# Layer 1 of a two-layer decoder: the low activations beside the high ones, one 512-column product with the high weights

## The chip, the core and the metric

The kernel runs on one core of a Trainium2 chip. TensorE (PE in the profile; its weight loads are PEld) multiplies, VectorE (DVE), ScalarE (ACT) and GpSimd (POOL) do the elementwise work, SyncE (SP) issues most DMAs. The metric is the device time in microseconds (us). Before the change it is 2330.26 us, the median of three runs (2329.82 to 2330.46).

## The reference

One sequence of 256 tokens, 16 meta tokens put in front (272 rows in all), width 2048, two layers, float32. Layer 0 works on all 272 rows. In layer 1 the shared K and V are made from all 272 rows, while queries, attention output and MLP are wanted for the 256 real tokens alone, since the output drops the meta rows.

```python
for layer in range(DEPTH):
    a = rms_norm(h, norm_attn[layer])
    if layer < N_A_LAYERS:
        ...
        o = forgetting_attention(split_heads(q), split_heads(k), split_heads(v), cum_logf)
        h = h + o.reshape(b, length, D_MODEL) @ fox_w_o[i]
    else:
        ...
        q = split_heads(a @ sb_w_q[i])
        o = stick_breaking_attention(q, shared_k, shared_v)
        h = h + o.reshape(b, length, D_MODEL) @ sb_w_o[i]
    h = h + squared_relu_mlp(rms_norm(h, norm_mlp[layer]), w_up[layer], w_down[layer])
return rms_norm(h, final_norm)[:, N_META:]
```

## The kernel before

Activations lie feature-major: 16 chunks of 128 features, each chunk 272 tokens wide (layer 1: 256). A float32 product is made of three products in the rounded type fp32r: an operand is split into a high part (ScalarE copies it into fp32r) and a low part (VectorE subtracts the high part from the original), and the kernel sums high weights x high activations, high weights x low activations, and low weights x high activations. The split of activations lives in a `Split` object: one SBUF tile with a row of 640 columns for each chunk, `hi` and `lo` views in it. `ROWS` says where in the row they start: for layer 1 (`t0 = M = 16`) hi at column 0 and lo at column 320.

Every weight matrix is worked off by `gemm_group` in column blocks of 512: four PSUM tiles `acc_<group>_<m>`, one whole bank each (512 float32 columns), for m = 0..3 of 128 output features. A group runs over four blocks kb of 512 input features. For each kb it loads two halves of raw weights (`raw`, on SP's queue), ScalarE makes `whi` (L222) and VectorE `wlo` (L223), each half 128 x 1024; `whi` and `wlo` have four buffers each, that is two kb ahead. Then TensorE runs 4 (m) x 4 (kc, chunks of 128 input features) triples of products, L175: for kb 0 and 3 one m after the other, four kc each; for kb 1 and 2 one half (two kc) after the other, all four m. In layer 1 (`t0` set) the series of each such run goes over all high-weight x hi products, then all high-weight x lo, then all low-weight x hi. After kb 3 of an m its `evac` takes the sum out of PSUM:

- query projection (4 groups): one VectorE operation into `qT1` (L522)
- output projection (4 groups) and MLP down projection (16 groups): `residual_add` into `hT` (L250)
- MLP up projection (16 groups): VectorE relu times the norm's factor (L486), ScalarE square (L488) and split high (L489), VectorE split low (L490)

The bank of `acc` m is used again by the next group's kb 0 at the same m, so an eviction has to be done three m's after the group's end at the latest. The four layer-1 K and V pairs of groups (`w_kv`) work on 272 columns and are layer-0-like.

The order on each engine is set by a scheduler with a timeline model; only TensorE's products of `gemm_group` are pinned to each other in the order in which they are written. Engines run their queues in order. `Norm.finish` (L156) puts one full-float32 product with 272 or 256 columns, two passes, between kb 1 and kb 2 of the first group after a norm.

Of the kernel before, what the change touches and what calls it, by code (L numbers as in the profile page):

```python
# [12 lines left out]
ALU = mybir.AluOpType  # L13
AX = mybir.AxisListType

P = 128
D = 2048
NC = D // P
M = 16
# [4 lines left out]
QSCALE = 1.0 / math.sqrt(P)  # L24
N_FF = 4

ROWS = {0: (48, 368), M: (0, 320)}
XROW = 640

G_A0, G_M0, G_KV, G_A1, G_M1, G_FIN = range(6)  # L30
# [3 lines left out]
def yoco_kernel(ctx: ExitStack, tc: tile.TileContext, hT_in, gains, b_f, w_f, w_qkv0, w_o0, w_up, w_dn,  # L34
# [83 lines left out]
    class Split:  # L118


        def __init__(self, label, t0):
            n = T - t0
            self.t0 = t0
            rows = xs.tile([P, NC * XROW + 64], F32R, tag="x", name=f"x_{label}")
            hi, lo = ROWS[t0]
            o = min(hi, lo)
            rows = rows[:, o:o + NC * XROW].rearrange("p (c t) -> p c t", c=NC)
            self.hi, self.lo = (rows[:, :, k - o:k - o + n] for k in (hi, lo))

    def split_chunk(sp, gi, c):  # L130

# [41 lines left out]
    def gemm_matmul(*args, **kw):  # L173

        ins = nc.tensor.matmul(*args, **kw).ins  # L175
        if queued and pinned[0]:
            tc.add_manual_dep(ins, queued[0].name, mybir.DependencyInfo(mybir.DependencyClass.NoSync,
                                                                        mybir.DependencyReason.DATA))
        queued[:] = [ins]

    def gemm_group(wblk, sp, t0, evac, before={}, after={}, load_x=None):

        uid[0] += 1
        u = uid[0]
        accs = [pacc.tile([P, 512], F32, tag="acc", name=f"acc_{u}_{m}") for m in range(4)]
        n = T - t0  # L190
        for kb in range(4):
            src_w = wblk[kb].rearrange("p (k c) -> p k c", k=4)
            if kb in before:
                before[kb]()
            piece = 1 if load_x is not None and kb < 2 else 2
            raws = [wraw.tile([P, 2, 512], F32, tag="raw", name=f"raw_{u}_{kb}_{hf}") for hf in range(2)]
            for k0 in range(0, 4, piece):
                if load_x is not None:
                    load_x(range(4 * kb + k0, 4 * kb + k0 + piece))
                if load_x is not None and kb == k0 == 0:  # L200

                    for c0 in (0, 256):
                        nc.scalar.dma_start(raws[0][:, 0, c0:c0 + 256], src_w[:, 0, c0:c0 + 256])
                else:
                    nc.sync.dma_start(raws[k0 // 2][:, k0 % 2:k0 % 2 + piece], src_w[:, k0:k0 + piece])
            parts = []
            for hf in range(2):
                whi = wspl.tile([P, 2 * 576], F32R, tag="whi", name=f"whi_{u}_{kb}_{hf}")
                wlo = wspl.tile([P, 2, 576], F32R, tag="wlo", name=f"wlo_{u}_{kb}_{hf}")
                if t0:  # L210
                    whi = whi.rearrange("p (k c) -> p k c", k=2)[:, :, 16:528]
                    wlo = wlo[:, :, 16:528]
                else:
                    whi = whi[:, :1024].rearrange("p (k c) -> p k c", k=2)
                    wlo = wlo[:, :, :512]
                boxes = [(o, piece, 0, 512) for o in range(0, 2, piece)]
                if load_x is not None and kb == hf == 0:
                    boxes[:1] = [(0, 1, 0, 256), (0, 1, 256, 512)]
                for o, no, c0, c1 in boxes:
                    src = raws[hf][:, o:o + no, c0:c1]  # L220
                    hp, lp = whi[:, o:o + no, c0:c1], wlo[:, o:o + no, c0:c1]
                    on_act = nc.scalar.activation(hp, src, AF.Copy)  # L222
                    on_dve = nc.vector.tensor_tensor(out=lp, in0=src, in1=hp.bitcast(F32), op=ALU.subtract)  # L223
                parts.append((whi, wlo))
            if kb in after:
                with tc.issue_after(on_act.ins), tc.issue_after(on_dve.ins):
                    after[kb]()


            if load_x is not None and kb == 0:  # L230
                runs = [([kc], range(4)) for kc in range(4)]
            elif kb in (0, 3):
                runs = [(range(4), [m]) for m in range(4)]
            else:
                runs = [(range(2 * hf, 2 * hf + 2), range(4)) for hf in range(2)]
            pinned[0] = load_x is None
            for kcs, ms in runs:
                if t0:
                    series = [(w, x, kc, m) for w, x in ((0, "hi"), (0, "lo"), (1, "hi")) for m in ms for kc in kcs]
                else:  # L240
                    series = [(w, x, kc, m) for m in ms for kc in kcs for w, x in ((0, "hi"), (0, "lo"), (1, "hi"))]
                for w, x, kc, m in series:
                    gemm_matmul(accs[m][:, :n], parts[kc // 2][w][:, kc % 2, m * P:(m + 1) * P],
                                getattr(sp, x)[:, 4 * kb + kc], start=kb == kc == w == 0 and x == "hi", stop=kb == kc == 3 and w == 1)
                if kb == 3:
                    for m in ms:
                        evac(m, accs[m][:, :n])

    def residual_add(c, acc, t0):
        nc.vector.tensor_tensor(out=hT[:, c, t0:], in0=acc, in1=hT[:, c, t0:], op=ALU.add)  # L250


    norm = Norm("a0", 0)
# [96 lines left out]
    for g in range(4):  # L350
# [2 lines left out]
        vT = att.tile([P, 4, T], F32, tag="vT", bufs=1, name=f"vT0_{g}")  # L353

        def evac_q(m, acc, qT=qT):
            nc.vector.scalar_tensor_tensor(out=qT[:, m, :], in0=acc, scalar=-QSCALE, in1=box["rstd"],
                                           op0=ALU.mult, op1=ALU.mult)

        def evac_kv(m, acc, t):
            nc.vector.tensor_tensor(out=t[:, m, :], in0=acc, in1=box["rstd"], op=ALU.mult)  # L360

        if g == 0:

            gemm_group(w_qkv0[0], xa, 0, lambda m, acc, qT=qT: nc.scalar.copy(qT[:, m, :], acc),
                       after={kb: (lambda kb=kb: first_norm(kb)) for kb in range(4)}, load_x=load_x)
            gate_products()
            box["rstd"] = norm.finish()
            for m in range(4):
                evac_q(m, qT[:, m, :])
            forget_gates(box["rstd"])  # L370
        else:
            gemm_group(w_qkv0[3 * g], xa, 0, evac_q)
# [100 lines left out]
    def mlp(layer, xm, norm, t0, last_evac):  # L473
        box = {}

        def get_rstd():
            box["r"] = norm.finish()

        for f in range(N_FF):
            u = Split(f"u{layer}_{f}", t0)  # L480
            for g in range(4):
                def evac(m, acc, g=g):
                    c = 4 * g + m
                    r = tmp.tile([P, T], F32, tag="relu", name=f"relu_{layer}_{f}_{c}")
                    u2 = tmp.tile([P, T], F32, tag="u2", name=f"u2_{layer}_{f}_{c}")
                    nc.vector.scalar_tensor_tensor(out=r[:, t0:], in0=acc, scalar=0.0, in1=box["r"][:, t0:],  # L486
                                                   op0=ALU.max, op1=ALU.mult)
                    nc.scalar.activation(u2[:, t0:], r[:, t0:], AF.Square)  # L488
                    nc.scalar.activation(u.hi[:, c], u2[:, t0:], AF.Copy)  # L489
                    nc.vector.tensor_tensor(out=u.lo[:, c], in0=u2[:, t0:], in1=u.hi[:, c].bitcast(F32),  # L490
                                            op=ALU.subtract)
                gemm_group(w_up[layer, f, g], xm, t0, evac, {2: get_rstd} if f == g == 0 else {})
            for g in range(4):
                def evac(m, acc, g=g):
                    residual_add(4 * g + m, acc, t0)
                    if f == N_FF - 1:
                        last_evac(4 * g + m)
                gemm_group(w_dn[layer, f, g], u, t0, evac)
# [20 lines left out]
    for g in range(4):  # L519
        def evac_q1(m, acc, g=g):  # L520
            q = qT1[g][:, m, :S]
            nc.vector.scalar_tensor_tensor(out=q, in0=acc, scalar=QSCALE, in1=box["rstd"][:, M:],  # L522
                                           op0=ALU.mult, op1=ALU.mult)
        def split_c(kb, g=g):
            for c in ([4 * kb + g - 1] if g < 3 else [4 * kb + 2, 4 * kb + 3]):
                split_chunk(xc, G_KV, c)

        gemm_group(w_q1[g], xq, M, evac_q1, {2: get_rstd1} if g == 0 else {},
                   after={kb: (lambda kb=kb: split_c(kb)) for kb in range(4)} if g else {})
# [192 lines left out]
```

## Time and profile before

| | |
|---|---|
| time, median of three runs | 2330.26 us |
| the profiled execution's own time | 2329.83 us |
| its span (first to last instruction) | 2328.0 us |
| granted TensorE clock, mean | 0.998 |
| TensorE products and weight loads | 19030 each |
| VectorE, ScalarE busy | 1289.9 us (55%), 1040.6 us (45%) |
| DMA moved | 412.32 MB, mean 177 GB/s |

The profile lists for each engine the busy time, the chain of work that ended last (which instruction released which, followed back from the end) and groups of instructions. Products on TensorE overlap their neighbours: a product's listed duration (some 280 ns) is longer than the distance to the next product, and the distance is what counts. It is read from the chain, where back-to-back products are merged into one entry with a count, or from two start times in the timeline. "x_a", "x_o", "x_m" and "x_u" are the `Split` tiles of query projection, output projection, MLP up and MLP down.

### The profile page before, as it was taken

To read this page: it belongs to the slowest core of one execution; us is meant where nothing else is said; L and a number is where in the kernel's file an instruction comes from. 1 tells how busy PE (TensorE), PEld (TensorE's weight loads), DVE (VectorE), ACT (ScalarE), POOL (GpSimd) and SP (SyncE) were. 2 spreads that over 40 slices of the span, in tenths; PEclk is the share of its full clock that TensorE was granted. 3 is DMA by queue.
4 is the path that set the end of the run, shared out by engine and by line. 5 is a ranking of instruction groups with operands and counts; after the bars stand their busy time and mean duration, and the time that the engine had idled before them with its cause. 6 is when DMAs were issued, how large, how long until landed. Compare 5 with 4: busy or idle time off the path is not lost.

```text
span 2328.0 us, 44800 instructions
## 1 busy us (share of the span) xinstructions
PE 2316.8 (100%) x19030; PEld 2309.8 (99%) x19030; DVE 1289.9 (55%) x1764; ACT 1040.6 (45%) x1397; POOL 38.4 (2%) x58
## 2 busy tenths in 40 slices
PE   9999999999999999999999999999999999999998
PEld 9999999999999999999999999999999999999998
DVE  7656556554455455455565555566555555555554
ACT  6444344443353344344544444455534434443553
POOL 1000000000000000000000000000000000000000
PEclk9999999999999999999999999999999999999999
DMA  7444545555555555555555444456565655656563
GB/s 240 166 163 157 181 154 168 185 174 180 181 170 185 172 184 177 183 170 184 173 188 183 156 153 149 152 180 199 180 192 178 194 182 184 195 182 191 179 192 127
DMA packets 116904, 412.32 MB, mean 177 GB/s; under 512 B 13520, under 2 KB 16992, under 8 KB 116704
## 3 DMA queue, kind: packets, MB, share of 16 engines
q1 hardware_dynamic: 114560, 406.29, 53.7%
q8 instruction: 149, 2.44, 0.4%
q10 hardware_dynamic: 2144, 3.17, 0.4%
q14 instruction: 51, 0.42, 0.1%
HBM read 407.29 MB, written 2.11 MB: 176 GB/s over the span
## 4 chain that ended last, share of the span: by engine, by line
PE 99%; DVE 0%; DMA 0%; ACT 0%; SPq 0%; issue 0%; DVEq 0%; ACTq 0%
PE acc L175 96%; PE ps L392 0%; PE pv L325 0%; PE pza L569 0%; PE po L454 0%; PE po L608 0%; DMA raw<-w_qkv 0%; PE po L609 0%; PE pzb L570 0%; PE po L455 0%; DVE ob L664 0%; PE pf L291 0%; PE pf L292 0%; PE pta L584 0%; PE pta L585 0%; PE pp L424 0%
## 5 line engine op out<-in xcount | busy, mean ns | idle before, releaser
L223 DVE TENSOR_TENSOR wlo<-raw,whi 128x1024 fp32r<-128x1024 f32 (+1 forms) x773 | 928.7, 1217 | 761.5 <-ACT whi L222 759.8
L222 ACT ACTIVATE whi<-raw 128x1024 fp32r<-128x1024 f32 (+1 forms) x773 | 796.5, 1049 | 1034.2 <-PE acc L175 1006.5
L175 PE MATMUL acc<-x_u,whi 128*128 128x272 f32 (+1 forms) x4096 | 651.9, 284 | 0.0
L175 PE MATMUL acc<-x_m,whi 128*128 128x272 f32 (+1 forms) x4096 | 651.7, 284 | 0.0
L175 PEld LDWEIGHTS acc<-x_u,whi 128*128 128x128 f32 x4096 | 573.9, 189 | 0.0
L175 PEld LDWEIGHTS acc<-x_m,whi 128*128 128x128 f32 x4096 | 573.6, 189 | 0.1
L175 PE MATMUL acc<-x_u,wlo 128*128 128x272 f32 (+1 forms) x2048 | 445.3, 284 | 0.0
L175 PE MATMUL acc<-x_m,wlo 128*128 128x272 f32 (+1 forms) x2048 | 445.2, 284 | 0.0
L175 PE MATMUL acc<-x_a,whi 128*128 128x272 f32 (+1 forms) x2048 | 361.8, 289 | 0.1
L175 PEld LDWEIGHTS acc<-x_u,wlo 128*128 128x128 f32 x2048 | 327.6, 189 | 0.0
L175 PEld LDWEIGHTS acc<-x_m,wlo 128*128 128x128 f32 x2048 | 327.5, 189 | 0.0
L175 PEld LDWEIGHTS acc<-x_a,whi 128*128 128x128 f32 x2048 | 303.4, 189 | 1.4 <-ACT whi L222 0.4
L175 PE MATMUL acc<-x_a,wlo 128*128 128x272 f32 (+1 forms) x1024 | 254.8, 287 | 0.0
L175 PE MATMUL acc<-x_kv,whi 128*128 128x272 f32 x1024 | 191.8, 288 | 0.0
L175 PEld LDWEIGHTS acc<-x_a,wlo 128*128 128x128 f32 x1024 | 176.5, 189 | 0.9 <-issue 0.5
L175 PE MATMUL acc<-x_o,whi 128*128 128x272 f32 (+1 forms) x1024 | 161.9, 282 | 0.0
L175 PEld LDWEIGHTS acc<-x_kv,whi 128*128 128x128 f32 x1024 | 159.7, 188 | 0.0
L175 PE MATMUL acc<-x_kv,wlo 128*128 128x272 f32 x512 | 147.5, 288 | 0.0
L175 PEld LDWEIGHTS acc<-x_o,whi 128*128 128x128 f32 x1024 | 141.7, 188 | 0.0
L250 DVE TENSOR_TENSOR hT<-acc,hT 128x272 f32<-128x272 f32 (+1 forms) x160 | 69.0, 431 | 88.1 <-PE acc L175 86.9
L175 PE MATMUL acc<-x_o,wlo 128*128 128x272 f32 (+1 forms) x512 | 110.5, 282 | 0.0
L175 PEld LDWEIGHTS acc<-x_kv,wlo 128*128 128x128 f32 x512 | 96.5, 188 | 0.0
(221 smaller groups left out, 969.2 us busy)
## 6 DMA issues: line engine op xcount, KB each, us to landing
raw<-w_up SPq DMA_DIRECT2D x256, 512.0 KB, 4.5
raw<-w_dn SPq DMA_DIRECT2D x256, 512.0 KB, 4.5
raw<-w_qkv SPq DMA_DIRECT2D x92, 512.0 KB, 3.8
raw<-w_o SPq DMA_DIRECT2D x64, 512.0 KB, 4.4
raw<-w_kv SPq DMA_DIRECT2D x64, 512.0 KB, 3.8
raw<-w_q SPq DMA_DIRECT2D x32, 512.0 KB, 4.5
fk<-f_dram ACTq DMA_DIRECT2D x4, 544.0 KB, 5.0
raw<-w_qkv SPq DMA_DIRECT2D x7, 256.0 KB, 4.5
```

The costliest lines, as they stand in the source:

```text
L175: ins = nc.tensor.matmul(*args, **kw).ins
L222: on_act = nc.scalar.activation(hp, src, AF.Copy)
L223: on_dve = nc.vector.tensor_tensor(out=lp, in0=src, in1=hp.bitcast(F32), op=ALU.subtract)
L250: nc.vector.tensor_tensor(out=hT[:, c, t0:], in0=acc, in1=hT[:, c, t0:], op=ALU.add)
```

## The change

In layer 1 lo now starts right behind hi (column 256 instead of 320), and `both` is a view of the 512 columns. Each run of `gemm_group` issues, for every m and kc, one product of the high weights with `both` into the whole bank, and after these one 256-column product of the low weights with hi, added to the bank's right half. The left half then holds high x high, the right half the two small terms. Evictions get a list of two halves in layer 1: `residual_add` adds both, one after the other, and `total` copies the right half to the target on ScalarE and adds the left half on VectorE, before the operation that was there. Layer 0 and the 272-column groups issue the same products in the same order as before.

```diff
-ROWS = {0: (48, 368), M: (0, 320)}
+ROWS = {0: (48, 368), M: (0, 256)}
...
+            if t0:
+                self.both = rows[:, :, :2 * n]
...
                 if t0:
-                    series = [(w, x, kc, m) for w, x in ((0, "hi"), (0, "lo"), (1, "hi")) for m in ms for kc in kcs]
+                    for m in ms:
+                        for kc in kcs:
+                            gemm_matmul(accs[m], parts[kc // 2][0][:, kc % 2, m * P:(m + 1) * P], sp.both[:, 4 * kb + kc],
+                                        start=kb == kc == 0, stop=False)
+                    for m in ms:
+                        for kc in kcs:
+                            gemm_matmul(accs[m][:, n:], parts[kc // 2][1][:, kc % 2, m * P:(m + 1) * P],
+                                        sp.hi[:, 4 * kb + kc], start=False, stop=kb == kc == 3)
...
                 if kb == 3:
                     for m in ms:
-                        evac(m, accs[m][:, :n])
+                        evac(m, [accs[m][:, :n]] + ([accs[m][:, n:]] if t0 else []))
 
     def residual_add(c, acc, t0):
-        nc.vector.tensor_tensor(out=hT[:, c, t0:], in0=acc, in1=hT[:, c, t0:], op=ALU.add)
+        for a in acc:
+            nc.vector.tensor_tensor(out=hT[:, c, t0:], in0=a, in1=hT[:, c, t0:], op=ALU.add)
+
+    def total(acc, to):
+
+        if len(acc) == 1:
+            return acc[0]
+        nc.scalar.copy(to, acc[1])
+        nc.vector.tensor_tensor(out=to, in0=acc[0], in1=to, op=ALU.add)
+        return to
...
-                    nc.vector.scalar_tensor_tensor(out=r[:, t0:], in0=acc, scalar=0.0, in1=box["r"][:, t0:],
+                    nc.vector.scalar_tensor_tensor(out=r[:, t0:], in0=total(acc, r[:, t0:]), scalar=0.0, in1=box["r"][:, t0:],
                                                    op0=ALU.max, op1=ALU.mult)
...
-            nc.vector.scalar_tensor_tensor(out=q, in0=acc, scalar=QSCALE, in1=box["rstd"][:, M:],
+            nc.vector.scalar_tensor_tensor(out=q, in0=total(acc, q), scalar=QSCALE, in1=box["rstd"][:, M:],
                                            op0=ALU.mult, op1=ALU.mult)
```

The lines of the changed kernel move: L175 becomes L178 (products), L222/L223 become L225/L226 (weight splits), L250 becomes L264, L486 to L490 become L508 to L512; L270 and L271 are the copy and the add in `total`.

First place, TensorE, kb 0 of group 83 (an up projection in layer 1), m = 0 and 1. Before:

```order
L175 MATMUL acc_83_0_22571<-x_m1_16818,whi_83_0_0_22579 128x256 x2
L175 MATMUL acc_83_0_22571<-x_m1_16818,whi_83_0_1_22583 128x256 x2
L175 MATMUL acc_83_0_22571<-x_m1_16818,whi_83_0_0_22579 128x256 x2
L175 MATMUL acc_83_0_22571<-x_m1_16818,whi_83_0_1_22583 128x256 x2
L175 MATMUL acc_83_0_22571<-x_m1_16818,wlo_83_0_0_22580 128x256 x2
L175 MATMUL acc_83_0_22571<-x_m1_16818,wlo_83_0_1_22584 128x256 x2
L175 MATMUL acc_83_1_22572<-x_m1_16818,whi_83_0_0_22579 128x256 x2
```

and now:

```order
L178 MATMUL acc_83_0_21067<-x_m1_16594,whi_83_0_0_21075 128x512 x2
L178 MATMUL acc_83_0_21067<-x_m1_16594,whi_83_0_1_21079 128x512 x2
L178 MATMUL acc_83_0_21067<-x_m1_16594,wlo_83_0_0_21076 128x256 x2
L178 MATMUL acc_83_0_21067<-x_m1_16594,wlo_83_0_1_21080 128x256 x2
L178 MATMUL acc_83_1_21068<-x_m1_16594,whi_83_0_0_21075 128x512 x2
```

Twelve products of 256 columns become four of 512 and four of 256; the columns that pass stay 3072, the weight loads go from twelve to eight.

Second place, VectorE at the end of group 82 (an up projection), the eviction of its last sum, `acc_82_3`. Before:

```order
L486 SCALAR_TENSOR_TENSOR relu_1_2_6_22547<-acc_82_2_22305,rstd_m1_18021 128x256
L490 TENSOR_TENSOR x_u1_2_22034<-u2_1_2_5_22530,x_u1_2_22034 128x256
L486 SCALAR_TENSOR_TENSOR relu_1_2_7_22565<-acc_82_3_22306,rstd_m1_18021 128x256
L223 TENSOR_TENSOR wlo_83_1_0_22640<-raw_83_1_0_22635,whi_83_1_0_22639 128x2x512
L223 TENSOR_TENSOR wlo_83_1_1_22644<-raw_83_1_1_22636,whi_83_1_1_22643 128x2x512
```

and now:

```order
L508 SCALAR_TENSOR_TENSOR relu_1_2_6_21043<-relu_1_2_6_21043,rstd_m1_17525 128x256
L226 TENSOR_TENSOR wlo_83_1_0_21120<-raw_83_1_0_21115,whi_83_1_0_21119 128x2x512
L512 TENSOR_TENSOR x_u1_2_20642<-u2_1_2_5_21028,x_u1_2_20642 128x256
L226 TENSOR_TENSOR wlo_83_1_1_21124<-raw_83_1_1_21116,whi_83_1_1_21123 128x2x512
L271 TENSOR_TENSOR relu_1_2_7_21059<-acc_82_3_20858,relu_1_2_7_21059 128x256
```

The operation that reads the group's last sum stood ahead of the next group's two low-weight splits and now stands behind both.

Third place, ScalarE at the same point, now (before, ScalarE did not read `acc` in layer 1):

```order
L270 COPY relu_1_2_6_21043<-acc_82_2_20857 128x256
L510 ACTIVATE u2_1_2_5_21028<-relu_1_2_5_21027 128x256
L225 ACTIVATE whi_83_1_0_21119<-raw_83_1_0_21115 128x2x512
L511 ACTIVATE x_u1_2_20642<-u2_1_2_5_21028 128x256
L225 ACTIVATE whi_83_1_1_21123<-raw_83_1_1_21116 128x2x512
L270 COPY relu_1_2_7_21059<-acc_82_3_20858 128x256
```

The copy of the last sum's right half stands behind the two high-weight splits, which in turn wait for TensorE to be done with group 82's last weights.

More of the change, by code (lines that the diff above doesn't have):

```diff
@@ L238, in gemm_group @@
                 if t0:
-                    series = [(w, x, kc, m) for w, x in ((0, "hi"), (0, "lo"), (1, "hi")) for m in ms for kc in kcs]
-                else:
[L241 to L244, printed above, removed]
+                    for m in ms:
[6 more added lines that the diff above has]
+                                        sp.hi[:, 4 * kb + kc], start=False, stop=kb == kc == 3)
+                else:
+                    for m in ms:
+                        for kc in kcs:
+                            wh, wl = (w[:, kc % 2, m * P:(m + 1) * P] for w in parts[kc // 2])
+                            hi, lo = sp.hi[:, 4 * kb + kc], sp.lo[:, 4 * kb + kc]
+                            gemm_matmul(accs[m][:, :n], wh, hi, start=kb == kc == 0, stop=False)
+                            gemm_matmul(accs[m][:, :n], wh, lo, start=False, stop=False)
+                            gemm_matmul(accs[m][:, :n], wl, hi, start=False, stop=kb == kc == 3)
                 if kb == 3:
                     for m in ms:
-                        evac(m, accs[m][:, :n])
+                        evac(m, [accs[m][:, :n]] + ([accs[m][:, n:]] if t0 else []))
     def residual_add(c, acc, t0):
-        nc.vector.tensor_tensor(out=hT[:, c, t0:], in0=acc, in1=hT[:, c, t0:], op=ALU.add)
+        for a in acc:
[6 more added lines that the diff above has]
+        return to
     norm = Norm("a0", 0)
@@ L355, in evac_q @@
         def evac_q(m, acc, qT=qT):
-            nc.vector.scalar_tensor_tensor(out=qT[:, m, :], in0=acc, scalar=-QSCALE, in1=box["rstd"],
+            nc.vector.scalar_tensor_tensor(out=qT[:, m, :], in0=acc[0], scalar=-QSCALE, in1=box["rstd"],
                                            op0=ALU.mult, op1=ALU.mult)
         def evac_kv(m, acc, t):
-            nc.vector.tensor_tensor(out=t[:, m, :], in0=acc, in1=box["rstd"], op=ALU.mult)
+            nc.vector.tensor_tensor(out=t[:, m, :], in0=acc[0], in1=box["rstd"], op=ALU.mult)
         if g == 0:
-            gemm_group(w_qkv0[0], xa, 0, lambda m, acc, qT=qT: nc.scalar.copy(qT[:, m, :], acc),
+            gemm_group(w_qkv0[0], xa, 0, lambda m, acc, qT=qT: nc.scalar.copy(qT[:, m, :], acc[0]),
                        after={kb: (lambda kb=kb: first_norm(kb)) for kb in range(4)}, load_x=load_x)
@@ L368, in yoco_kernel @@
             for m in range(4):
-                evac_q(m, qT[:, m, :])
+                evac_q(m, [qT[:, m, :]])
             forget_gates(box["rstd"])
```

## The prediction

> **What bounds the kernel now.** I read the page's busy table and its chain first, to see which engine the end hangs on.
>
> ```profile
> PE 2316.8 (100%) x19030; PEld 2309.8 (99%) x19030; DVE 1289.9 (55%) x1764; ACT 1040.6 (45%) x1397; POOL 38.4 (2%) x58
> PE 99%; DVE 0%; DMA 0%; ACT 0%; SPq 0%; issue 0%; DVEq 0%; ACTq 0%
> ```
>
> TensorE never waits; the time is the number of products times their distance. A change is worth what it does to that distance, or what it makes TensorE wait. So I looked for distances in the chain in order of time (start, length, what, count), where an unbroken run of products is one entry.
>
> ```profile
> 439.91 756.83 PE acc L175 x6144
> 1196.73 0.46 PE pms_a L156 x2
> 1197.19 106.54 PE acc L175 x894
> 1512.87 89.07 PE acc L175 x785
> 1601.93 0.43 PE pms_m L156 x2
> 1602.36 708.08 PE acc L175 x6012
> ```
>
> Layer 0's MLP, 272 columns: 756.83 / 6144 = 123.2 ns for each product. Layer 1's output projection, 256 columns: 89.07 / 785 = 113.5. Layer 1's MLP, 256 columns too: 708.08 / 6012 = 117.8. The reader is to see that 256 columns have two paces. The long one begins at the full-float32 product of the norm (pms_m) and never goes away; the query projection behind pms_a has it as well (of its 894 products 222 are the K projection's of 272 columns, 222 x 0.1232 = 27.3 us; 79.2 us for the other 672 is again 117.8). Layer 1 has 40 groups x 64 = 2560 triples. Short are the output projection's 256 and the halves of two groups ahead of pms_a and pms_m, 32 each, 320 in all; the other 2240 are long. A triple costs 3 x 117.8 = 353.3 ns at the long pace, 3 x 113.5 = 340.4 at the short one.
>
> **TensorE, part one: the wide product.** Nothing in layer 1's groups has 512 columns, but the stick-breaking attention has fp32r products of that width, between the group's own (timeline; start, length, then what):
>
> ```profile
> 1501.97 0.39 PE L584 MATMUL pta<-eh,ntri_r 128*128 128x512 f32 x1
> 1502.20 0.29 PE L588 MATMUL ptb<-eh,ntri_r 128*128 128x288 f32 x1
> ...
> 1503.59 0.39 PE L585 MATMUL pta<-el,ntri_r 128*128 128x512 f32 x1
> 1503.82 0.30 PE L586 MATMUL pta<-eh,nones_r 128*128 128x288 f32 x1
> ...
> 1504.21 1.09 PE L175 MATMUL acc<-x_o,whi 128*128 128x256 f32 x8
> 1505.14 0.62 PE L175 MATMUL acc<-x_o,wlo 128*128 128x256 f32 x4
> 1505.59 0.51 PE L175 MATMUL acc<-x_o,whi 128*128 128x256 f32 x3
> ```
>
> From a 512's start to the next start it is 0.23 us both times; the chain has the same for another:
>
> ```profile
> 1319.09 0.23 PE pta L584
> ```
>
> So 230 ns, 225 to 235 by the rounding. These read two pieces of 256, not 512 columns in a row, so they are the nearest row and not the same thing. A line through 272 columns at 123.2 and 512 at 230 has 0.445 ns a column and 2.2 ns fixed; at 256 it gives 116.1, between the two paces. So a 512 is not cheaper than two products at the short pace (227) and some 5 ns cheaper than two at the long one (235.6).
>
> **TensorE, part two: the 256-column product that stays.** It now follows wide ones in runs of four (kb 0 and 3) or eight (kb 1 and 2). The last fence shows what 256 columns do behind wider products: eight from 1504.21 to 1505.14 are 116 each, the next four, 0.45 us, 113. The first four of the eight then have 0.93 - 4 x 0.1135 = 0.48 us, 119 each. Half of the products stand in runs of four (119), half in runs of eight (116): I take 117.6. The pace that pms sets is lost at the first wide product, and each run starts anew. Ends: 113.5 and 119.
>
> A triple is then 230 + 117.6 = 347.6 ns. Where the pace was long a triple wins 5.7 ns, 2240 x 5.7 = 12.8 us; where it was short it loses 7.2, 320 x 7.2 = 2.3 us. TensorE's sum is -10.5 us. With the ends of both terms a triple goes from 338.5 to 354, which is -33.8 to +5.9 us.
>
> The Trainium skill, "TensorE: Matmul & The Clock Gate", section "Back-to-back issue gap", gives N/2.4 + 2.5 ns between products, so 109.2 for 256 columns and 215.8 for 512. By that rule a product saved is worth its fixed 2.5 ns alone, 2560 x 2.5 = 6.4 us as an estimate, and it speaks against a larger gain; the trace is above it at both widths.
>
> **The evictions.** `total` adds a ScalarE copy and a VectorE add for 80 sums, `residual_add` one VectorE add for 80 sums. Prices from the groups by form, MLP of layer 1 (mean ns of one ahead of the second bar):
>
> ```profile
> L223 DVE TENSOR_TENSOR wlo<-raw,whi 128x1024 fp32r<-128x1024 f32 x250 | 300.7, 1223 | 245.7 <-ACT whi L222 245.2
> L250 DVE TENSOR_TENSOR hT<-acc,hT 128x256 f32<-128x256 f32 x60 | 25.5, 425 | 37.8 <-PE acc L175 36.6
> L490 DVE TENSOR_TENSOR x_u<-u,x_u 128x256 fp32r<-128x256 f32 x64 | 25.3, 416 | 0.0
> ...
> L222 ACT ACTIVATE whi<-raw 128x1024 fp32r<-128x1024 f32 x249 | 256.4, 1054 | 331.4 <-PE acc L175 331.4
> L489 ACT ACTIVATE x_u<-u 128x256 fp32r<-128x256 f32 x64 | 26.5, 413 | 1.5
> ```
>
> 160 adds at 0.425 are 68 us of VectorE, 80 copies at 0.41 are 33 us of ScalarE. Both engines are idle about half of that stretch, waiting for TensorE to free weight buffers:
>
> ```profile
> 1602.36:2310.44 708.08, 708.08 (x6016) 708.08 (x6014) 379.03 (x453) 314.70 (x402) 0.00 (x0) 1.00 0.57 184
> ```
>
> (VectorE 379 and ScalarE 315 of 708 us.) The work is hidden as long as a bank is free when the next group wants it. The tight one is `acc` 3 of an up projection. Its copy now stands behind both high-weight splits of the next kb 1 on ScalarE, its add behind both low-weight splits on VectorE; behind them wait the relu of m 3 and the next splits, and TensorE. The splits start when TensorE frees the weights, just before the group's end E:
>
> ```profile
> 1952.20 2.01 ACT L222 ACTIVATE whi<-raw 128x1024 fp32r<-128x1024 f32 x2 [4.83 <-PE acc L175]
> ...
> 1952.91 0.43 DVE L250 TENSOR_TENSOR hT<-acc,hT 128x256 f32<-128x256 f32 x1 [0.99 <-PE acc L175]
> ```
>
> There the pair starts 0.7 us ahead of the read of the last sum. Now copies and squares of m 2 and m 1 come first, so I take E - 0.4. First split to E + 0.65, x_u high to E + 1.1, second split to E + 2.1; on VectorE the first low split runs to about E + 1.95, x_u low to 2.4, the second low split to 3.6, the add to 4.05. TensorE wants the bank after three m's of the next group, 12 triples: E + 4.17. That fits by about 0.1 us, with a handover to pay; I put 0.05 us on 16 up groups, 0.8 us. Down and output projections have no ScalarE copy, their second add waits for one low split less and is done near E + 2.1; the query groups' add comes with less between the splits. All these cost nothing. If the cover were gone, each 0.1 us of delay would cost 1.6 us over the up groups.
>
> **The tail** is not covered: the last chunk's eviction is in the chain, and a second add goes behind it, +0.43 us.
>
> ```profile
> 2315.59 0.44 DVE hT L250
> ```
>
> **Sum:** -10.5 + 0.8 + 0.4 = -9.3 us, against the profiled execution's 2329.83 (span 2328.0): span 2318.7, execution 2320.5. The median, 0.43 us above that execution, goes to 2321.0.
>
> **Rivals.** A measurement of this kernel tells a change from none at about 0.2%, 4.7 us: 2325.6 and 2334.9 are the marks.
>
> Short pace everywhere. The wide product leaves the next weight load all the time it wants, and 512 costs two at the short pace, 227, with 113.5 for the other: 340.4 a triple, 2240 x 12.9 = 28.9 us less, 2302.6 with the eviction's 1.2. For it: 113.5 occurs over 768 products in a row. Against it: three measured 512s at 230, and the first four behind wide products at 119.
>
> Only the fixed part goes. Each stretch keeps its pace, and a product saved is worth 2.2 ns: 2560 x 2.2 = 5.6 us, 2325.9 with evictions. For it: the long pace lasted 6012 products through every change of tile. Against it: 256-column products leave it behind wide ones. The Trainium skill's rule above is this mechanism, with 6.4 us, 2325.1.
>
> Columns alone, long pace throughout. 512 costs 235.6 and the 256 never recovers: 2240 triples gain nothing, 320 lose 12.9 ns, 4.1 us; 2335.6. For it: the paces do stick. Against it: 512s at 230.
>
> `acc` 3 late, the other side. ScalarE and VectorE take their queues in order, and if the last sum is read one low split later than I reckon (1.2 us), TensorE stands 1.1 to 1.2 us at m 3 of each group behind an up or a query projection, 20 x 1.2 = 24 us: 2321 - 0.8 + 24 = 2344. For it: the margin is 0.1 us, and the chain E to E + 4.05 goes through two engines four times. Against it: the weights are freed earlier now than I assumed if products are shorter. It decides against the change from 14 / 20 = 0.7 us of lateness on.
>
> **How the numbers follow.** Forecast 0.54 (its own range 2312 to 2327, triples from 344 to 350); short pace 0.10; only the fixed part 0.12; columns alone 0.09; `acc` 3 late 0.15. Faster: 0.47 of the forecast, 0.10, and 0.03 of the fixed part, 0.60. Same: 0.07, 0.09 and 0.04 of columns alone, 0.20. Slower: 0.05 and 0.15, 0.20. The range is 2303 to 2337: it takes in short pace and columns alone, and leaves out most of the late bank.
>
> **What would show it.** In the chain after: the MLP of layer 1 as a run of some 4000 products, half of them 512 wide, with 347.6 / 2 = 174 ns a product; 170 is short pace, 176 and above columns alone. In the timeline: starts 0.23 apart behind a 512, the first 256s of a run further apart than the last. In the waits: no TensorE idle time released by VectorE's L271; 16 or more such waits near 1 us are the late bank. The tail one add longer. I am wrong if 512 columns in a row do not cost what two pieces of 256 cost, or if the chain shows VectorE between products.

## The result and the profile after

The changed kernel takes 2317.28 us, the median of four runs (2317.01 to 2319.15); the kernel before, on the same chip, 2330.36 us (2329.82 to 2331.12). The ratio is 0.9945, with a 95% interval from 0.9928 to 0.9963: 13.1 us less, where 9.3 had been forecast. The profiled execution took 2317.01 us, its span is 2315.3.

The busy table of the changed kernel's page, and the shares of its chain by engine:

```profile
PE 2304.6 (100%) x16470; PEld 2183.7 (94%) x16470; DVE 1349.5 (58%) x1924; ACT 1063.8 (46%) x1477; POOL 40.5 (2%) x58
PE 99%; DVE 0%; DMA 0%; ACT 0%; issue 0%; DVEq 0%; ACTq 0%
```

2560 products and as many weight loads are gone, and VectorE has 160 operations more, ScalarE 80. TensorE sets the end as before. The chain of waits in order of time (start, length, what, count):

```profile
439.81 757.03 PE acc L178 x6112
1197.30 105.09 PE acc L178 x670
...
1514.92 87.48 PE acc L178 x506
...
1602.84 694.77 PE acc L178 x4008
2297.61 0.34 PE pms_fin L643 x4
```

Layer 1's MLP is 708.08 us before and 694.77 now. That is 694.77 / 2004 = 346.7 ns for each triple (one product of 512 columns and one of 256) in place of 353.3, and 13.31 us less. The span is 12.7 us shorter; the rest nearly balances. From pms_a's start to the end of the query projection's run it was 107.00 us (1196.73 to 1303.73) and is 105.55 (1196.84 to 1302.39), 1.45 less. From there to pms_m's end it was 298.63 and is 300.45, 1.82 more; this holds the output projection, at the short pace before. What lies ahead of these and behind the MLP is 0.24 longer.

The two products' sizes are in the timeline of the changed kernel (start, length, then what):

```profile
1801.49 1.07 PE L178 MATMUL acc<-x_m,wlo 128*128 128x256 f32 x8
1802.40 2.02 PE L178 MATMUL acc<-x_m,whi 128*128 128x512 f32 x8
1804.27 1.07 PE L178 MATMUL acc<-x_m,wlo 128*128 128x256 f32 x8
1805.18 1.09 PE L178 MATMUL acc<-x_m,whi 128*128 128x512 f32 x4
```

From the first 512 to the first 256 behind it are 1.87 us, 234 ns for each; eight 256s take 0.91 us, 114 each. Finer, from one start to the next in ns, worked out from the start times of the trace for one run of four and one of eight in that MLP:

```
512: 226 236 231 236     256: 118 113 114 113
512: 226 236 231 236 231 235 231 236     256: 118 114 113 113 114 113 113 114
```

So the 256s are at the short pace but for the first of a run. The first 512 of a run costs two products at the short pace (227), the others go by turns at 236, two at the long one (235.6), and at 231. Over the whole MLP the mean 512 is 232.4 and the mean 256 is 114.3. Forecast were 230 and 117.6: each is off, and the sum by 1 ns.

### The profile page after: what moved, and what is told of

Read it like the earlier page. It is cut to its first block, busy times and chain, and to the rows that moved or that the text cites. A ratio compares the mean times of both kernels' runs of the same rounds, so it can differ in the third digit from the quotient of the medians.

```text
span 2315.3 us, 39918 instructions
## 1 busy us (share of the span) xinstructions
PE 2304.6 (100%) x16470; PEld 2183.7 (94%) x16470; DVE 1349.5 (58%) x1924; ACT 1063.8 (46%) x1477; POOL 40.5 (2%) x58
## 4 chain that ended last, share of the span: by engine, by line
PE 99%; DVE 0%; DMA 0%; ACT 0%; issue 0%; DVEq 0%; ACTq 0%
PE acc L178 96%; PE ps L414 0%; PE pv L347 0%; PE pza L591 0%; PE po L476 0%; PE po L630 0%; PE pzb L592 0%; PE po L631 0%; DMA raw<-w_qkv 0%; PE po L477 0%; DVE ob L686 0%; PE pf L313 0%; PE pf L314 0%; PE pms_fin L643 0%; PE pta L606 0%; PE pta L607 0%
## 5 line engine op out<-in xcount | busy, mean ns | idle before, releaser
L226 DVE TENSOR_TENSOR wlo<-raw,whi 128x1024 fp32r<-128x1024 f32 (+1 forms) x773 | 932.3, 1217 | 737.4 <-ACT whi L225 733.5
L225 ACT ACTIVATE whi<-raw 128x1024 fp32r<-128x1024 f32 (+1 forms) x773 | 800.1, 1050 | 965.7 <-PE acc L178 932.2
L178 PE MATMUL acc<-x_m,whi 128*128 128x272 f32 (+1 forms) x3072 | 648.6, 323 | 0.0
L178 PE MATMUL acc<-x_u,whi 128*128 128x272 f32 (+1 forms) x3072 | 648.2, 323 | 0.0
L178 PEld LDWEIGHTS acc<-x_m,whi 128*128 128x128 f32 x3072 | 497.3, 188 | 28.2
L178 PEld LDWEIGHTS acc<-x_u,whi 128*128 128x128 f32 x3072 | 497.3, 188 | 28.0
L178 PE MATMUL acc<-x_m,wlo 128*128 128x272 f32 (+1 forms) x2048 | 441.7, 282 | 0.0
L178 PE MATMUL acc<-x_u,wlo 128*128 128x272 f32 (+1 forms) x2048 | 441.6, 282 | 0.0
L178 PE MATMUL acc<-x_a,whi 128*128 128x272 f32 (+1 forms) x1792 | 361.0, 306 | 0.1
L178 PEld LDWEIGHTS acc<-x_m,wlo 128*128 128x128 f32 x2048 | 338.7, 188 | 17.4
L178 PEld LDWEIGHTS acc<-x_u,wlo 128*128 128x128 f32 x2048 | 338.7, 188 | 17.4
L178 PEld LDWEIGHTS acc<-x_a,whi 128*128 128x128 f32 x1792 | 284.4, 189 | 8.4 <-ACT x_a L136 0.4
L178 PE MATMUL acc<-x_a,wlo 128*128 128x272 f32 (+1 forms) x1024 | 254.2, 286 | 0.0
L178 PE MATMUL acc<-x_kv,whi 128*128 128x272 f32 x1024 | 191.8, 288 | 0.0
L178 PEld LDWEIGHTS acc<-x_a,wlo 128*128 128x128 f32 x1024 | 179.4, 188 | 5.3 <-issue 0.5
L178 PE MATMUL acc<-x_o,whi 128*128 128x272 f32 (+1 forms) x768 | 162.9, 323 | 0.0
L178 PEld LDWEIGHTS acc<-x_kv,whi 128*128 128x128 f32 x1024 | 159.7, 188 | 0.0
L178 PE MATMUL acc<-x_kv,wlo 128*128 128x272 f32 x512 | 147.5, 288 | 0.0
L264 DVE TENSOR_TENSOR hT<-acc,hT 128x256 f32<-128x256 f32 (+1 forms) x240 | 102.8, 428 | 71.4 <-PE acc L178 69.7
L178 PEld LDWEIGHTS acc<-x_o,whi 128*128 128x128 f32 x768 | 124.1, 188 | 6.8
L178 PE MATMUL acc<-x_o,wlo 128*128 128x272 f32 (+1 forms) x512 | 111.0, 283 | 0.0
L178 PEld LDWEIGHTS acc<-x_kv,wlo 128*128 128x128 f32 x512 | 96.4, 188 | 0.0
```

The lines of the kernel that those rows point to most:

```text
L264: nc.vector.tensor_tensor(out=hT[:, c, t0:], in0=a, in1=hT[:, c, t0:], op=ALU.add)
```

## The experiments

All times are medians in us, against runs of the kernel before on the same chip, whose median lay between 2330.17 and 2330.48 throughout. The granted TensorE clock is 0.998 in every profiled run, so it is no part of the differences. "..." in an edit stands for lines left out.

**Is it the products saved, or the pace?** The kernel before, with two products of 512 columns more in the whole program: one ahead of kb 3 of the query projection's first group and one ahead of kb 3 of layer 1's first MLP group, each reading hi and lo as two pieces of 256, into a bank that nothing reads.

```diff
+            if t0:
+                self.two = rows.rearrange("p c (h t) -> p c h t", h=2)[:, :, :, :n]
...
+            if t0 and before and kb == 3:
+                wide = patt.tile([P, 2, 256], F32, tag="patt", name=f"wide_{u}")
+                gemm_matmul(wide, parts[0][0][:, 0, :P], sp.two[:, 0], start=True, stop=True)
             for kcs, ms in runs:
```

> The kernel before with nothing of the change, and one extra 512-wide product (high weights with hi and lo, result not used) ahead of kb 3 of the query projection's and the MLP's first group in layer 1. Theory, the pace of 256-column products is set by what came last, and a wide product ends the long pace: behind it they go on at 113.4 ns instead of 117.8 to the end of the stretch, some 6620 products x 4.4 = 29 us less, 0.5 us for the two extra products: 2302 us. Rival, the change won through the weight loads it saves: none is saved here, 2330.8. Rival, the long pace belongs to these stages (their tiles, their DMA and split work): it comes back behind the extra product, 2330.8.

2301.43 (2301.13 to 2301.61), ratio 0.9876 (0.9862 to 0.9891): 28.9 us less than before and 15.9 less than the change, with every weight load still there. Its chain:

```profile
1202.47 98.12 PE acc L177 x846
...
1509.72 89.07 PE acc L177 x785
...
1605.11 675.93 PE acc L177 x5964
```

The MLP's products are 675.93 / 5964 = 113.3 ns apart, before 117.8; the output projection, at the short pace already, has its 89.07 us to the digit. One product ended the long pace, and nothing brought it back for 5964 products. The same with lo at column 256 and the extra product reading 512 columns in a row:

```diff
-ROWS = {0: (48, 368), M: (0, 320)}
+ROWS = {0: (48, 368), M: (0, 256)}
...
+                wide = patt.tile([P, 512], F32, tag="patt", name=f"wide_{u}")
+                gemm_matmul(wide, parts[0][0][:, 0, :P], sp.both[:, 0], start=True, stop=True)
```

> As the run with one extra wide product, but with lo at column 256, so that the extra product reads its 512 columns in one piece instead of two with a gap; same place, weights and bank. A single wide product in one piece, first of a sum, left the long pace as it was (2334.0); this tells what differs. If the two pieces are what ends the long pace: it stays here, 2330.8 us. If it is the place in the order, the weights or the bank: 2301.5.

2302.70 in two runs, ratio 0.9880 (0.9860 to 0.9899), the MLP again 675.93 us for 5964 products. One piece or two is the same. And with an extra product that is only 256 wide, the rest as in the first of these:

```diff
...
+                gemm_matmul(wide[:, 0, :], parts[0][0][:, 0, :P], sp.hi[:, 0], start=True, stop=True)
```

> As the run with one extra wide product, but the extra product has 256 columns (hi alone, its own bank). Theory, the width is what ends the long pace: it stays at 117.8, 2330.5 us. Rival, any extra product (another bank, a shifted order) ends it: 2302.

2330.26, ratio 1.0000 (0.9990 to 1.0011). Its MLP behind the extra product:

```profile
1608.42 702.43 PE acc L177 x5964
```

That is 117.8 ns still. A product more, a bank more, or their place does nothing: it is the width.

**Do fewer weight loads help by themselves?** The changed kernel with the same products, but each 512 followed by its 256, not in runs:

```diff
-                    for m in ms:
-                        for kc in kcs:
                             gemm_matmul(accs[m][:, n:], parts[kc // 2][1][:, kc % 2, m * P:(m + 1) * P],
                                         sp.hi[:, 4 * kb + kc], start=False, stop=kb == kc == 3)
```

> The changed kernel with each 512-wide product followed at once by its 256-column one, in place of runs of four or eight of a width. In the changed kernel a 512 behind a 256 took 226 ns, the later ones of a run 231 to 236, and the first 256 of a run 118, the others 113.4. Theory, the distance depends on the neighbour's width alone: 226 + 118 = 344 a triple in place of 346.7, 2560 x 2.7 = 7 us less than the changed kernel, 2310. Rival, every change from wide to narrow costs the 236 that the last 512 of a run took: 236 + 118 = 354, 2335.

2334.08, ratio 1.0016 (1.0007 to 1.0026), where my theory had 2310. The rival's sum, 236 + 118 ns a triple, had it. Page and chain:

```profile
PE 2321.2 (100%) x16470; PEld 2195.0 (94%) x16470; DVE 1343.3 (58%) x1924; ACT 1061.8 (46%) x1477; POOL 40.7 (2%) x58
```

```profile
1606.38 708.08 PE acc L178 x4008
```

This MLP has a third fewer products and loads than before's and the same 708.08 us: 235 for the 512 and 118 for the 256, a triple of 353.3. So 2004 products and weight loads saved gain nothing where the long pace stays. The change's gain hangs on the order of its products, in runs.

**Do lo's place, one piece, or the evictions matter?** Before with lo at column 256 alone (the first line of the diff), and the changed kernel with lo back at 320 and its 512 columns read in two pieces:

> The kernel before with lo at column 256 of a row instead of 320, nothing else. Theory: where lo lies has no part in the gain, the MLP of layer 1 stays at 117.8 ns a product, 2330.3 us. Rival, the place of lo alone shortens or lengthens the distance: the gain (13 us) or a part of it shows here, or a loss that the change had to make up for.

> The changed kernel with lo back at column 320: the wide product reads hi and lo as two pieces of 256 with a gap of 64 columns. Theory, the place of lo has no part in it: 2317.3 us, the MLP at 694.8 us for 4008 products. Rival, 512 columns in one piece are what makes the wide product cheap or dear: more than 2 us off either way.

2330.47, ratio 1.0001 (0.9991 to 1.0010), and 2317.26, ratio 0.9947 (0.9930 to 0.9964), which is the change's own time. "Right behind the high ones" has no part in it.

For the evictions, before's products with the change's evictions: `residual_add` and `total` get the same sum twice, so layer 1's sums come out doubled. Against before, beside the change's own `residual_add` and `total`:

```diff
...
-                        evac(m, accs[m][:, :n])
+                        evac(m, [accs[m][:, :n]] + ([accs[m][:, :n]] if t0 else []))
```

> The kernel before with the change's evictions: the same sum is handed to them twice (ScalarE copy and VectorE add, or two adds), so layer 1's sums come out doubled; the products are those of before. Theory: the evictions are hidden but for the last one, +0.4 to +1.2 us, 2330.8 to 2331.5. Rival, they cost the predicted late bank or more: 3 us and up, with TensorE idle time released by VectorE's add.

2330.27, ratio 1.0001 (0.9991 to 1.0010). Its page and its chain:

```profile
PE 2317.3 (100%) x19030; PEld 2309.4 (99%) x19030; DVE 1349.5 (58%) x1924; ACT 1065.5 (46%) x1477; POOL 40.5 (2%) x58
```

```profile
1602.40 708.08 PE acc L178 x6012
```

All 240 operations more are there and the MLP has the length of before's. The medians are 2330.27 and 2330.28; the profiled span is 0.9 us longer than before's, less than the 2 us over which the runs spread, so no price of theirs shows.

**What starts the long pace?** Before with one full-float32 product of 256 columns ahead of kb 3 of the output projection's first group, a stretch at the short pace:

```diff
+            if full is not None and kb == 3:
+                ps = patt.tile([P, 512], F32, tag="patt", name=f"full_{u}")
+                gemm_matmul(ps[:, :n], mean_w, full, start=True, stop=True)
...
-            gemm_group(w[g], ao, t0, evac)
+            gemm_group(w[g], ao, t0, evac, full=hT[:, 8, M:] if t0 and g == 0 else None)
```

> The kernel before with one extra full-float32 product of 256 columns (like the norm's, result not used) ahead of kb 3 of the output projection's first group in layer 1, a stretch that ran at 113.5 ns. Theory, a full-float32 product starts the long pace: the 720 products from there to the norm's own one go at 117.8, 3.1 us more and 0.4 for the product itself, 2333.8. Rival, the long pace comes from the MLP's work: the stretch stays at 113.5, 2330.7.

2334.06, ratio 1.0016 (1.0006 to 1.0027). The chain:

```profile
1519.98 0.43 PE full L175 x2
1520.42 84.80 PE acc L175 x720
1605.22 0.43 PE pms_m L156 x2
1605.65 708.08 PE acc L175 x6012
```

84.80 / 720 = 117.8 where it was 113.5. So a full-float32 product that meets the short pace starts the long one, and pms_a and pms_m, products of this kind, stand where it starts in before. Here pms_m meets the long pace already, and it stays: 708.08 us for 6012 products.

**How many wide products does it take?** The changed kernel with 512 columns only for the first product of each sum, all others 256 wide:

```diff
-                            gemm_matmul(accs[m], parts[kc // 2][0][:, kc % 2, m * P:(m + 1) * P], sp.both[:, 4 * kb + kc],
-                                        start=kb == kc == 0, stop=False)
+                            if kb == kc == 0:
+                                gemm_matmul(accs[m], parts[0][0][:, 0, m * P:(m + 1) * P], sp.both[:, 0], start=True, stop=False)
+                            else:
+                                gemm_matmul(accs[m][:, :n], parts[kc // 2][0][:, kc % 2, m * P:(m + 1) * P],
+                                            sp.hi[:, 4 * kb + kc], start=False, stop=False)
+                                gemm_matmul(accs[m][:, n:], parts[kc // 2][0][:, kc % 2, m * P:(m + 1) * P],
+                                            sp.lo[:, 4 * kb + kc], start=False, stop=False)
```

> The changed kernel with its evictions and its two halves of a bank, but only the first product of a sum is 512 wide; the other 15 of 16 are 256 wide, high weights with hi and then with lo. Theory: the wide product drops the long pace, everything behind it goes at 113.4, a triple costs 340.2, and the evictions stay hidden: 2302 to 2303 us, like the kernel before with one extra wide product (2301.4). Rival, it is the many wide products that win: with one in sixteen the gain of the change falls to a sixteenth, about 2329. Rival, evictions late: at this pace a bank is wanted 0.08 us earlier than in the changed kernel, TensorE would show idle time released by VectorE's add, 2304 and more.

2334.03, ratio 1.0016 (1.0007 to 1.0025), a miss by 31 us. The chain:

```profile
1606.49 708.03 PE acc L178 x5888
```

The first one behind pms_m did end the long pace, and the second, eleven products on, started it again; the others left it as it was. In ns from start to start, from the trace's start times (the eight behind each 512):

```
512: 234   256: 121 116 114 114 113 113 114 113
512: 225   256: 119 117 118 117 119 117 118 118
512: 236   256: 118 118 117 118 118 117 118 118
```

The same product with its columns in two pieces (lo at 320):

> One wide product as first of each sum, as before, but with lo at column 320, read in two pieces. If the two pieces are what ends the long pace: 113.4 ns behind each, 2302 to 2303 us. If not: the long pace stays, 2334.

2334.24, ratio 1.0017 (1.0006 to 1.0027), with the same 708.03 us. Then the first two products of each sum wide, lo at 256 again; the edit against the kernel with one:

```diff
-                            if kb == kc == 0:
-                                gemm_matmul(accs[m], parts[0][0][:, 0, m * P:(m + 1) * P], sp.both[:, 0], start=True, stop=False)
+                            if kb == 0 and kc < 2:
+                                gemm_matmul(accs[m], parts[0][0][:, kc, m * P:(m + 1) * P], sp.both[:, kc], start=kc == 0, stop=False)
```

> The first two products of a sum 512 wide, in one piece, behind each other; the other 14 of 16 as 256 and 256. In the changed kernel every run of four or eight wide products ends with 231, 236 and then 256 columns at 118, 113, 113. If it is two or more wide ones in a row that leave the short pace behind them: 226, 236, 118 and then 113.4, some 2.1 us over all sums more than a kernel at the short pace throughout, with hidden evictions 2303 to 2304 us. If only the longer runs do it, or a pair acts as a single one: the long pace, 2334.

2304.20, ratio 0.9886 (0.9869 to 0.9902). Its chain:

```profile
1600.57 683.45 PE acc L178 x5764
```

Behind pms_m's long pace the first pair (234 and 233 ns apart) ends it; every later pair (226 and 236) meets the short pace and hands it on, where a single one does not. All the change's evictions are in this kernel too, 13 us below the change, and stay hidden.

**Where, or how often?** Before's products with sixteen probes in layer 1's MLP, whose sums go nowhere. The table says at which group and kb one stands; "next" is a 512 in a bank of its own with the next product's weights, "other" one with other weights, "sum" and "sums" go to the bank that the next product opens, "full" is a full-float32 product as above.

```diff
+    PROBES = {2: (3, "next"), 4: (3, "next"), 6: (3, "full"), 8: (3, "other"), 10: (3, "full"), 12: (1, "next"), 14: (3, "full"),
+              16: (0, "sum"), 18: (3, "full"), 20: (0, "next"), 22: (3, "full"), 24: (0, "sums"), 26: (3, "full")}
...
```

> Before's products, with probes in layer 1's MLP, whose sums go nowhere: seven places get extra 512-column products (hi x both pieces), and two groups behind each, ahead of kb 3, one full-float32 product starts the long pace again. In order: (1) ahead of kb 3 of group 2, in a bank of its own, with the next product's weights; (2) the same ahead of kb 3 of group 4, where the pace should then be short already; (3) group 8, kb 3, with other weights than the next product's; (4) group 12, kb 1, next product's weights; (5) group 16, ahead of kb 0 in the bank that the next product opens; (6) group 20, ahead of kb 0 in a bank of its own; (7) group 24, one ahead of each m of kb 0, in that sum's bank. The extra products cost 2.4 + 1.5 = 3.9 us; all stretches long gives 2334.2, all short 14.1 less. Theory 1, a bank of its own decides: 1 to 4 and 6 are followed by 113.5 ns, 5 and 7 by 117.8: 2324.7. Theory 2, the next product's weights decide: all short but 3. Theory 3, the place kb 3 decides: 1, 2 and 3 short, 4 to 7 long: 2329.1. Theory 4, each single wide product changes the pace to the other one: 1 short, behind 2 long, 3 to 6 short, 7 (four of them) long. Theory 5, one in a sum every 11 products is what holds the long pace in e5_one_wide: all short but 7.

2325.08 (2324.16 to 2326.83, eight runs), ratio 0.9978 (0.9966 to 0.9989). The chain, from pms_m on:

```profile
1601.87 50.88 PE acc L177 x432
1652.75 0.23 PE wide L177
1652.98 43.53 PE acc L177 x384
1696.52 0.23 PE wide L177
1696.74 45.23 PE acc L177 x384
1741.97 0.43 PE full L177 x2
1742.40 43.54 PE acc L177 x384
1785.94 0.23 PE wide L177
1786.16 45.23 PE acc L177 x384
1831.39 0.43 PE full L177 x2
1831.82 32.66 PE acc L177 x288
1864.48 0.23 PE wide L177
1864.70 56.53 PE acc L177 x480
1921.24 0.43 PE full L177 x2
...
2011.30 0.43 PE full L177 x2
2011.73 27.22 PE acc L177 x240
2038.94 0.23 PE wide L177
2039.17 62.19 PE acc L177 x528
```

Divide each length by its count: 117.8, then 113.4, 117.8, 113.4, 117.8, 113.4, 117.8, and so on. Every probe changed the pace to the other one, the wide ones and the full-float32 ones alike, at kb 0, 1 and 3, in a bank of its own or the sum's, with either choice of weights. That is the fourth theory. But I had taken the full product for one that always leads to the long pace, so the stretches of the third to the sixth wide probe came out the other way round: five of the six full products met the long pace and ended it. The four of "sums" alternate as well, 225 and 231 ns wide, with 118 ns behind the first and third and 113 behind the second and fourth. Theories on the bank, the weights and the place fall.

The fourth theory does not hold beyond these probes, though. In all runs a single wide or full product that met the short pace between 256s started the long one. One that met the long pace did not always end it: not the later single ones above, and not pms_m, which met the long pace in the alternating kernel, in both with one wide product for each sum and in the one with the added full product, and left it long each time.

## Why the prediction was right, and where its sizes were off

**What bounds it.** Right: TensorE, without a wait, and the count of products times their distance.

**The two paces.** Right that the time is in the pace and that pms starts the long one: an added full product did the same. The prediction had "The pace that pms sets is lost at the first wide product". It takes a little more: behind pms_m the first eight 512s, and the eight 256s after them (117 to 119 ns), are still at the long pace; the next eight 512s are 233 to 234 apart, and the 256s behind them reach 113. And it hangs on the order, for which the prediction had no reason: the change's own products by turns keep the long pace to the end (2334.08). That its wide products stand in runs was luck as far as the prediction goes.

**The triple.** Forecast 230 + 117.6 = 347.6 ns, measured 232.4 + 114.3 = 346.7, as from the chain. The step that was mis-sized is the 256-column product: I took "119" for the first four behind wide ones, from a rounded 0.48 us, and it is 118 for the first alone. The 512 was 2.4 ns too low: the attention's 512s, at 230, are single ones between other products, and in a run all but the first cost 231 to 236. The two errors point opposite ways, so that the sum was nearer than its terms. The 0.9 ns on 2560 triples are 2.3 us.

**The evictions.** Forecast 0.8 us for `acc` 3; none was seen: the trace has no TensorE wait in layer 1's MLP. The changed kernel's timeline at the end of an up group, E = 1658.19, for those that set it:

```profile
1657.59 1.05 ACT L225 ACTIVATE whi<-raw 128x1024 fp32r<-128x1024 f32 x1
...
1658.19 1.09 PE L178 MATMUL acc<-x_m,whi 128*128 128x512 f32 x4
...
1658.85 1.05 ACT L225 ACTIVATE whi<-raw 128x1024 fp32r<-128x1024 f32 x1
...
1659.80 0.36 ACT L270 COPY relu<-acc 128x256 f32<-128x256 f32 x1
...
1661.29 0.42 DVE L271 TENSOR_TENSOR relu<-acc,relu 128x256 f32<-128x256 f32 x1
...
1662.35 1.09 PE L178 MATMUL acc<-x_m,whi 128*128 128x512 f32 x4
```

The copy and the add stand behind both splits, as forecast. The bank is read by E + 3.52 and TensorE opens it at E + 4.16, so the cover is 0.64 us, not 0.1: the first split starts at E - 0.6, 0.2 us earlier than I had assumed, and the splits follow one another closer. The tail's second add does not lengthen the end by 0.43 either; from the first pms_fin in the chain on it is 17.69 us against 17.56. Together with the triple that is the whole difference: 2.3 + 0.8 + 0.3 = 3.4 us of the forecast 9.3 to the span's 12.7.

**The rivals.** Two of them occurred, in other kernels. "Short pace everywhere" (2302.6) is what two 512-column products make of before: 2301.43. "Columns alone, long pace throughout" (2335.6) is what the change's own products give in alternating order: 2334.08. "Only the fixed part goes" is ruled out by the same run at the long pace, where 2004 loads fewer in the MLP changed nothing. The Trainium skill, "TensorE: Matmul & The Clock Gate", section "Back-to-back issue gap", has N/2.4 + 2.5 ns as the gap of isolated products, and says that it counts too much for streams with weight loads at large N. By the formula the change would have gained 6.4 us as an estimate. The trace agrees with neither: 113.3 or 117.8 ns at 256 columns and 226 to 236 at 512 are both above the formula's 109.2 and 215.8. `acc` 3 late did not occur.

**What the change is, then.** Measured against the short pace it loses: 346.7 ns a triple against 3 x 113.3 = 340.0, 2004 x 6.7 = 13.4 us in the MLP alone. It gains only because before runs that MLP at the long pace, and its wide products in runs of four and eight end at the short one. The version to keep is before with the two extra products.

**What stays open** is why there are two paces, and when a single product that meets the long pace ends it. Weights, bank, place and pieces are excluded, since the first single wide product behind pms_m, like the later ones in all four, did end it where the later ones did not. What differs is how many 256-column products stand between it and the wide or full product ahead of it: 12, 48, 96, 384, 432, 480 and 528 where the long pace ended, 1, 10, 58 and 154 where it stayed. The former are all multiples of twelve and the latter are not; but pms_m, 720 behind the added full product, left it long too, so the count is not the whole condition. It may be a hidden phase of the long pace; that is not shown, since no run varied the count alone.

## What to carry to other kernels

Where TensorE is the bound and never waits, divide the length of each unbroken run in the chain by its count, and compare stretches of the same shape: a different distance for the same product is a loss that no busy share shows. Look at what stood at the border between the two, here one full-float32 product of a norm, and try the cheapest thing that could put the pace back before rewriting the products themselves. Then read from the chain whether the pace stayed: here a second product of the same kind could bring the long one back. An edit that removes instructions can gain for another reason than the instructions removed; the same products in another order (here 2334 against 2317 us) tell the two apart.

## What the runs showed of the hardware

Products of fp32r data with 256 columns follow one another at 113.3 or at 117.8 ns, and keep either for as long as nothing else comes between: 5964 and 6012 products in a row, through every change of tile, weights and bank. A single 512-column product, or a full-float32 one of 256 columns, ended the short pace wherever it met it between 256s, and changed the pace in all sixteen probes; but single 512s 11 and 155 products apart, and a full one 720 products behind another, left the long pace as it was. Two 512s in a row hand on the short pace. 272-column products have one pace, some 123 ns, in all these kernels. A 512-column product is hardly cheaper than its two halves: 225 to 226 ns behind the short pace, where two 256s take 226.6, and 231 to 236 behind the long one (two 256s 235.6) or another 512. And with a third fewer weight loads, at the long pace, the MLP took 708.08 us, the same to the last digit.
